# Reciprocal square roots, mask additions and the decay rows' transfers move from GpSimd to VectorE and to the weights' loading queue, in a hybrid decoder block

## The chip, the cores and the metric

The kernel runs on one core of a Trainium2 chip. A core has a matrix engine (TensorE, PE in the profile, with its weight loads as PEld), a vector engine (VectorE, DVE), a scalar engine (ScalarE, ACT), GpSimd (POOL) and SyncE (SP), which issues transfers. Each works off its own instructions in a fixed order and waits for the others by semaphores. The metric is the time of one execution on the device in microseconds (us); less is better.

## The reference

One decoder block over 256 tokens of 2048 channels, in float32: a half-weighted SwiGLU feed-forward, a token mixer, a second feed-forward, a gated per-layer embedding and a last norm.

```python
h = h + 0.5 * swiglu(rmsnorm(h, ffn1_norm), ffn1_w_gate, ffn1_w_up, ffn1_w_down)
proj = rmsnorm(h, mix_norm) @ w_in
o_gdn = gdn_mixer(...)          # 8 heads of 128: convolution, silu, l2norm, gated delta rule, rmsnorm, gate
o_ssm = ssd_mixer(...)          # 16 heads of 64: convolution, silu, chunked state space, gate, rmsnorm
h = h + concat([o_gdn, o_ssm]) @ w_out
h = h + 0.5 * swiglu(rmsnorm(h, ffn2_norm), ffn2_w_gate, ffn2_w_up, ffn2_w_down)
h = h + sigmoid(rmsnorm(h, ple_norm) @ ple_w_gate) * rmsnorm(p @ ple_w_proj, ple_post_norm)
return rmsnorm(h, final_norm)
```

Both mixers need `decay = exp(where(j <= i, gc_i - gc_j, -inf))`, with `gc` the cumulated logs of one head, and the delta rule needs the inverse of a lower triangular matrix `I + lower` per chunk and head. All norms need `x * rsqrt(mean(x * x) + EPS)`.

## The kernel before

**Products.** Weights are stationary. `load` (line 107) brings one column tile of 1 MB through SyncE's queue into one of three buffers `raw`; `split` (line 113) makes a rounded part `hi` on ScalarE (line 118) and the rest `lo` on VectorE (line 119), in pieces of 1024 columns, four buffers each; `chain` (line 122) multiplies both (lines 128, 130, 132), and `total_of` adds the two sums up. This goes on from the first stage to the last. A transfer for `raw` can be issued only when VectorE has made `lo` of the tile that lay there.

**Work beside the products.** The recurrent parts are generators in the list `side`; `tick` (line 174) advances each of them by one step after each piece of a product. The framework then settles the order of each engine's instructions ahead of the run with a simulated timeline; on the chip each engine keeps to that order.

**Per-token scalars** (`scalars`, line 408): at their end the cumulated logs are written as rows to DRAM (`rows<-gct`, line 447, on GpSimd's queue).

**Decay.** `spread` (line 483) loads rows of `gc_i` onto all partitions into one of two buffers `dec` (line 486, GpSimd's queue, 256 KB); `decay` (line 490) adds the causal mask on GpSimd (line 492, 128x512) and exponentiates on ScalarE (line 494). There are 12 of each: one for each of the four pairs of delta-rule heads, two for each of the four quads of state-space heads. A quad also loads `er` twice (line 727, GpSimd's queue, 8 in all).

**Delta rule** (`gdn_pair`, line 500), four pairs in turn. VectorE makes `LA` from `k k^T` and the decay (line 533). The diagonal blocks go through DRAM, on SyncE's queue (`blkl<-LA`, line 554, then `Lb<-blkl`, line 556). GpSimd solves them by substitution in 31 steps of two instructions (`tb`, line 582, and `Z`, line 584); Lb, Z and tb have one buffer. The result goes back through DRAM (`blky<-Z`, line 585, `Y<-blky`, line 592), and VectorE transposes it (`oT<-Y`, line 595). Products on TensorE follow (lines 606 and 635).

**Reciprocal square roots.** `rsq` (line 207) takes the power -0.5 on GpSimd (line 210) and refines it by one Newton step on VectorE (lines 212 to 214). It is called 16 times: six times for the norms over tokens (`stats`, line 220, of `ffn` twice, `mix`, `ple`, `post` and `final`), twice for the state-space groups (`sn`), and twice per pair of delta-rule heads (`rs`, line 543, and `ro`, line 671).

Of the kernel before, what the change touches and what calls it, by code (L numbers as in the profile page):

```python
# [10 lines left out]
F32R = mybir.dt.float32r  # L11
AF = mybir.ActivationFunctionType
# [17 lines left out]
# columns of the parameter pack  # L30
# [12 lines left out]
# the inverse: diagonal blocks of BS, CG columns of one per partition, then doubled  # L43
# [4 lines left out]
# columns of the constant pack: identity, upper triangle, additive causal mask, level masks, unit columns  # L48
# [7 lines left out]
def constant_pack():  # L56
# [5 lines left out]
    # the columns of the identity that the partition holds, partition = (block, group of columns)  # L62
# [6 lines left out]
def tile_hybrid_block(ctx, tc, xT, pT, con, par, wgu1, wd1, wnar, win, wout, wgu2, wd2, wproj, wple, outT):  # L69
# [30 lines left out]
    # ---------------------------------------------------------------- helpers  # L100
# [6 lines left out]
    def load(src):  # L107
        """One transfer of the stationary tiles [P, n * 128] of one column tile."""
        raw = rawp.tile([P, 2048], F32, tag="raw", name="raw")
        nc.sync.dma_start(raw[:, :src.shape[-1]], src)  # L110
        return raw

    def split(src):
        """hi + lo = src exactly, each of them wide enough for one pass."""
# [7 lines left out]
    def chain(ps, hi, lo, act_in, ks, first=True, last=True):  # L122
        """ps[:, 0] (+)= (hi + lo) @ high part, ps[:, 1] (+)= hi @ low part of act_in, for the tiles w of
        hi + lo and the tiles k of act_in."""
# [10 lines left out]
    def single(src, act_in, ks):  # L135
        """The product as a whole in ps[:, 0]."""
# [14 lines left out]
    def product(srcs, act_in, ks, out):  # L151
        """out = the product of the column tile that lies in the transfers srcs, rows ks, with act_in."""
# [18 lines left out]
    # work that runs beside the products: each generator is advanced by one step after each piece  # L171
# [14 lines left out]
    def split_x(k, wname):  # L186
        """The parts of xs are those of h * w, for one k tile."""
# [5 lines left out]
    def split_into(dst, src):  # L193
        """dst[:, :, 0] + dst[:, :, 1] = src exactly."""
        act.copy(dst[:, :, 0, :], src)
        dve.tensor_tensor(out=dst[:, :, 1, :], in0=src, in1=dst[:, :, 0, :].bitcast(F32), op=ALU.subtract)

    def sumsq(acc, src, first):
        """acc[P, 2, T] += src^2, src a pair of tiles."""
# [7 lines left out]
    def rsq(m, n, name):  # L207
        """1/sqrt(m) for a [P, n] tile."""
        y = small.tile([P, n], F32, tag=f"rsq{n}", name=name)
        pool.tensor_tensor(out=y, in0=m, in1=mhalf[:, :n], op=ALU.pow)  # L210
        t = small.tile([P, n], F32, tag=f"rsqt{n}", name=name + "t")
        dve.tensor_tensor(out=t, in0=y, in1=y, op=ALU.mult)
        dve.scalar_tensor_tensor(out=t, in0=t, scalar=-0.5, in1=m, op0=ALU.mult, op1=ALU.mult)
        dve.scalar_tensor_tensor(out=y, in0=t, scalar=1.5, in1=y, op0=ALU.add, op1=ALU.mult)
        return y

    mhalf = cp.tile([P, 16], F32, name="mhalf")
    pool.memset(mhalf, -0.5)

    def stats(squares, width, name, use, wait=2):  # L220
        """use(row): 1/sqrt(mean over width channels + eps) per token, as a row on every partition (in PSUM).
        squares: [P, T] tiles whose sum over partitions and tiles is the sum of squares."""
# [29 lines left out]
    # ---------------------------------------------------------------- loads  # L252
    warm = small.tile([P, 1], F32, tag="warm", name="warm", bufs=1)
    act.activation(warm, ones[:, 0:1], AF.Silu)
    # the array's clock rises with use: multiply while the first transfers are on their way
# [5 lines left out]
    # the first transfers alternate between the tokens and the first three column tiles  # L261
# [28 lines left out]
    # ---------------------------------------------------------------- feed-forward  # L290
    def ffn(wgu, wd, squares, next_name, start=None):
        """h += 0.5 * swiglu(rmsnorm(h)); squares: gives those of h; returns those of the new h."""
# [50 lines left out]
    # ---------------------------------------------------------------- token mixer  # L343
    with ExitStack() as mix:
# [5 lines left out]
        # halved conv weights and bias: silu(2u) = u * (1 + tanh(u))  # L350
# [13 lines left out]
        # a pair of projected tiles, behind three columns of zeros  # L364
# [8 lines left out]
        # ---- per-token scalars: a (8), dt (16), b (8) -> decay logs, dt, beta  # L373
        raw = load(wnar)
        ps = mm_bank("nar")
        for k in range(0, KD, 8):
            # both parts as columns of one stationary tile: rows 0-31 and 32-63 of the product
# [30 lines left out]
        def scalars():  # L408
# [9 lines left out]
            # log(1 + e) = 2 atanh(e / (2 + e))  # L418
# [24 lines left out]
            # the cumulated logs as rows, in DRAM to be spread over the partitions from there  # L443
# [3 lines left out]
            nc.gpsimd.dma_start(rows.rearrange("c n i -> (c n) i"), gct)  # L447
# [6 lines left out]
        # ---- projection of a pair of column tiles, causal conv, silu  # L454
# [18 lines left out]
        def silu_gate(w0):  # L473
            """Twice the silu."""
# [8 lines left out]
        def spread(src):  # L483
            """Rows of gc_i on every partition."""
            d = m2.tile([P, 4, P], F32, tag="dec", name="dec")
            nc.gpsimd.dma_start(d.rearrange("p (c n) i -> p c n i", c=src.shape[0]),  # L486
# [3 lines left out]
        def decay(d, c):  # L490
            """exp(gc_i - gc_j) for j <= i, else 0, as [j, n, i]; d: rows of gc_i, c: columns of -gc_j."""
            pool.tensor_tensor(out=d, in0=d, in1=over(cmask, 4), op=ALU.add)  # L492
# [3 lines left out]
        # scratch for the diagonal blocks and their inverses  # L496
        blocks = [[tc.dram_tile([4 * (P // BS), BS, BS], F32, name=f"blk{n}{i}") for n in "ly"] for i in range(2)]

        # ---- gated delta rule, two heads at a time; matrices in the order (chunk, head)
        def gdn_pair(i, KQ, V):  # L500
# [12 lines left out]
            # squares of k (the diagonal of k k^T) and of q by token  # L513
# [424 lines left out]
def _rows(v):  # L938
    """[n * 128] -> [128, n]."""
    return v.reshape(-1, P).T  # L940
# [61 lines left out]
```

## Time and profile before

| | us |
|---|---|
| median of 3 runs | 2117.88 (2116.24 to 2119.15) |
| span of the profiled execution | 2115.8 |
| TensorE busy | 2064.8 |
| VectorE busy | 1351.4 |
| ScalarE busy | 1047.7 |
| GpSimd busy | 256.7 |

The span runs from the first to the last instruction of one profiled execution. The median is 2.1 us above it. A busy time is the time in which the engine had at least one instruction under way. The mixer lies between about 760 and 1165 us of the span; the feed-forwards lie before and behind it.

### The profile page before, as it was taken

Reading aid. Unit: us, or ns where it says so; the run is one execution under the profiler, and the core shown is the slowest. Engines: PE = TensorE matmul, PEld = TensorE weight load, DVE = VectorE, ACT = ScalarE, POOL = GpSimd, SP = SyncE. Lnnn points to the kernel's source line nnn. Section 1 sums busy time; section 2 is a strip of 40 time slices with the busy share of each in tenths; the row PEclk is TensorE's granted clock in tenths of the full one; section 3 lists DMA queues with packets and bytes.
Section 4 is the critical chain, followed back from the end, with each engine's and each line's share of the span. In section 5 each row is a group of like instructions: output and inputs, shape, how many; then the busy total and the mean of one; then the engine's idle time right before and its main releaser. Section 6 shows DMA issues by size and latency. Waiting matters only on the chain.

```text
span 2115.8 us, 29521 instructions
## 1 busy us (share of the span) xinstructions
PE 2064.8 (98%) x11824; PEld 1795.9 (85%) x11824; DVE 1351.4 (64%) x1908; ACT 1047.7 (50%) x1591; POOL 256.7 (12%) x368
## 2 busy tenths in 40 slices
PE   9999999999999999888989999999999999999997
PEld 7888888888888888777878888888888888888886
DVE  7655555656556677767777666665555556556685
ACT  6444444444445555444455556544444444445554
POOL 2000000000000011667540011000000000000011
PEclk9999999999999999998999999999999999999998
DMA  7555455555545555434544555555456555545652
GB/s 261 187 182 195 158 190 184 207 191 188 182 172 179 190 198 164 163 123 148 168 137 151 194 179 187 191 189 190 163 183 211 185 193 180 190 160 190 201 194 101
DMA packets 67129, 380.77 MB, mean 180 GB/s; under 512 B 11744, under 2 KB 13024, under 8 KB 33840
## 3 DMA queue, kind: packets, MB, share of 16 engines
q1 hardware_dynamic: 65664, 374.93, 52.3%
q0 software_dynamic: 1328, 3.97, 1.0%
q8 instruction: 92, 1.51, 0.3%
q14 instruction: 45, 0.37, 0.1%
HBM read 376.21 MB, written 2.65 MB: 179 GB/s over the span
## 4 chain that ended last, share of the span: by engine, by line
PE 85%; POOL 7%; DMA 3%; issue 2%; DVE 2%; SPq 0%; ACT 0%; POOLq 0%; DVEq 0%; ACTq 0%
PE mm L130 55%; PE mm L128 26%; POOL Z L584 3%; POOL tb L582 3%; PE mm L132 2%; DMA Lb<-blkl 1%; DMA blkl<-LA 1%; DMA er<-rows 1%; DVE lo L119 1%; DMA Y<-blky 0%; PE pj L130 0%; DMA hT<-in_xT 0%; DVE LA L533 0%; POOL dec L486 0%; POOL dec L492 0%
## 5 line engine op out<-in xcount | busy, mean ns | idle before, releaser
L130 PE MATMUL mm<-xs,hi 128*128 128x512 f32 x3888 | 1367.0, 399 | 1.8 <-ACT hi L118 1.8
L119 DVE TENSOR_TENSOR lo<-raw,hi 128x1024 fp32r<-128x1024 f32 (+1 forms) x774 | 864.2, 1124 | 489.8 <-ACT hi L118 489.4
L128 PE MATMUL mm<-xs,lo 128*128 128x256 f32 x3645 | 1028.8, 282 | 6.4 <-DVE lo L119 6.4
L118 ACT CAST hi<-raw 128x1024 fp32r<-128x1024 f32 (+1 forms) x774 | 745.7, 964 | 517.7 <-PE mm L130 403.5
L130 PEld LDWEIGHTS mm<-xs,hi 128*128 128x128 f32 x3888 | 718.5, 189 | 155.9 <-ACT hi L118 2.3
L128 PEld LDWEIGHTS mm<-xs,lo 128*128 128x128 f32 x3645 | 687.5, 189 | 20.8 <-DVE lo L119 8.4
L130 PE MATMUL mm<-hid,hi 128*128 128x512 f32 x1408 | 492.5, 397 | 0.0
L128 PE MATMUL mm<-hid,lo 128*128 128x256 f32 x1344 | 377.8, 281 | 0.0
L130 PEld LDWEIGHTS mm<-hid,hi 128*128 128x128 f32 x1408 | 260.2, 188 | 59.0
L205 POOL TENSOR_TENSOR acc<-acc,sq 128x512 f32<-128x512 f32 x43 | 65.6, 1525 | 1602.3 <-ACT sq L204 1578.0
L128 PEld LDWEIGHTS mm<-hid,lo 128*128 128x128 f32 x1344 | 253.3, 188 | 3.0
L168 ACT COPY t<-mm 128x256 f32<-128x256 f32 x167 | 62.4, 374 | 158.5 <-PE mm L130 157.6
L169 DVE TENSOR_TENSOR t<-t,mm 128x256 f32<-128x256 f32 x167 | 69.9, 419 | 85.7 <-ACT t L168 85.4
L168 ACT COPY s<-mm 128x256 f32<-128x256 f32 x88 | 32.8, 373 | 148.2 <-PE mm L130 148.1
L130 PE MATMUL mm<-osp,hi 128*128 128x512 f32 x256 | 88.9, 396 | 0.0
L169 DVE TENSOR_TENSOR s<-s,mm 128x256 f32<-128x256 f32 x88 | 37.1, 421 | 73.7 <-ACT s L168 73.6
L132 PE MATMUL mm<-xs,lo 128*128 128x256 f32 x243 | 69.6, 286 | 11.7 <-DVE lo L119 11.7
L584 POOL TENSOR_TENSOR Z<-Z,tb 128x124 f32<-128x124 f32 (+30 forms) x124 | 67.8, 547 | 9.4
L128 PE MATMUL mm<-osp,lo 128*128 128x256 f32 x240 | 67.1, 281 | 0.0
L132 PEld LDWEIGHTS mm<-xs,lo 128*128 128x128 f32 x243 | 45.9, 189 | 24.5 <-DVE lo L119 14.1
L582 POOL TENSOR_TENSOR tb<-Lb,Z 128x124 f32<-128x124 f32 (+30 forms) x124 | 61.7, 498 | 27.0 <-DMA Lb<-blkl 17.9
L130 PEld LDWEIGHTS mm<-osp,hi 128*128 128x128 f32 x256 | 46.9, 188 | 10.1
(296 smaller groups left out, 1091.4 us busy)
## 6 DMA issues: line engine op xcount, KB each, us to landing
raw<-in_wgu SPq DMA_DIRECT2D x173, 1024.0 KB, 4.8
raw<-in_wd SPq DMA_DIRECT2D x128, 704.0 KB, 4.1
raw<-in_win SPq DMA_DIRECT2D x52, 1024.0 KB, 5.0
raw<-in_wout SPq DMA_DIRECT2D x16, 1024.0 KB, 4.9
raw<-in_wple SPq DMA_DIRECT2D x16, 1024.0 KB, 4.8
first<-in_wgu SPq DMA_DIRECT2D x12, 256.0 KB, 7.2
dec<-rows POOLq DMA_DIRECT2D x12, 256.0 KB, 4.7
Lb<-blkl SPq DMA_DIRECT2D x4, 512.0 KB, 5.2
```

The source lines that it names most:

```text
L118: act.copy(hi, src)
L119: dve.tensor_tensor(out=lo, in0=src, in1=hi.bitcast(F32), op=ALU.subtract)
L128: pe.matmul(ps[:, 0, :], lo[:, w, :], act_in[:, k, 0, :], start=False, stop=False, skip_group_check=True)
L130: pe.matmul(ps, hi[:, w, :], act_in[:, k], start=start, stop=stop, skip_group_check=True)
L132: pe.matmul(ps[:, 0, :], lo[:, w, :], act_in[:, k, 0, :], start=False, stop=False, skip_group_check=True)
L168: act.copy(out, ps[:, 0, :])
L169: dve.tensor_tensor(out=out, in0=out, in1=ps[:, 1, :], op=ALU.add)
L205: pool.tensor_tensor(out=acc, in0=acc, in1=sq, op=ALU.add)
L582: pool.tensor_tensor(out=t, in0=over(Lb[:, j, j + 1:], CG), in1=Z[:, :, j:j + 1].to_broadcast([P, CG, n]), op=ALU.mult)
L584: pool.tensor_tensor(out=Z[:, :, j + 1:], in0=Z[:, :, j + 1:], in1=t, op=ALU.subtract)
```

## The change

- `rsq` no longer uses GpSimd. A first guess is made on the bits of the number with two VectorE instructions (shift, then subtract from a constant), and three Newton steps of three VectorE instructions follow, in place of one power and one step. The tile `mhalf` and its memset go.
- `decay` adds the mask on VectorE.
- The write of the rows (line 447) and the loads of `dec` (line 486) and `er` (line 727) are issued by SyncE.

The rest of the difference is comments that were taken out.

```diff
 def rsq(m, n, name):
     y = small.tile([P, n], F32, tag=f"rsq{n}", name=name)
-    pool.tensor_tensor(out=y, in0=m, in1=mhalf[:, :n], op=ALU.pow)
     t = small.tile([P, n], F32, tag=f"rsqt{n}", name=name + "t")
-    dve.tensor_tensor(out=t, in0=y, in1=y, op=ALU.mult)
-    dve.scalar_tensor_tensor(out=t, in0=t, scalar=-0.5, in1=m, op0=ALU.mult, op1=ALU.mult)
-    dve.scalar_tensor_tensor(out=y, in0=t, scalar=1.5, in1=y, op0=ALU.add, op1=ALU.mult)
+    dve.tensor_scalar(t.bitcast(I32), m.bitcast(I32), 1, None, op0=ALU.logical_shift_right)
+    dve.tensor_scalar(y.bitcast(I32), t.bitcast(I32), -1.0, float(0x5F3759DF), op0=ALU.mult, op1=ALU.add)
+    for _ in range(3):
+        dve.tensor_tensor(out=t, in0=y, in1=y, op=ALU.mult)
+        dve.scalar_tensor_tensor(out=t, in0=t, scalar=-0.5, in1=m, op0=ALU.mult, op1=ALU.mult)
+        dve.scalar_tensor_tensor(out=y, in0=t, scalar=1.5, in1=y, op0=ALU.add, op1=ALU.mult)
     return y
-mhalf = cp.tile([P, 16], F32, name="mhalf")
-pool.memset(mhalf, -0.5)
...
-    nc.gpsimd.dma_start(rows.rearrange("c n i -> (c n) i"), gct)
+    nc.sync.dma_start(rows.rearrange("c n i -> (c n) i"), gct)
...
 def spread(src):
     d = m2.tile([P, 4, P], F32, tag="dec", name="dec")
-    nc.gpsimd.dma_start(d.rearrange("p (c n) i -> p c n i", c=src.shape[0]),
+    nc.sync.dma_start(d.rearrange("p (c n) i -> p c n i", c=src.shape[0]),
                         src.unsqueeze(0).to_broadcast([P, *src.shape]))
...
 def decay(d, c):
-    pool.tensor_tensor(out=d, in0=d, in1=over(cmask, 4), op=ALU.add)
+    dve.tensor_tensor(out=d, in0=d, in1=over(cmask, 4), op=ALU.add)
...
     for hh in range(2):
-        nc.gpsimd.dma_start(er[64 * hh:64 * hh + 64],
+        nc.sync.dma_start(er[64 * hh:64 * hh + 64],
                             rows[1, 8 + h0:12 + h0, :].rearrange("(j h) l -> h j l", h=2)[hh:hh + 1]
                             .to_broadcast([64, 2, P]))
```

## Rows read from the trace of the kernel before

**Rows 1.** The page, part 1: busy time, share of the span, instructions.
```profile
PE 2064.8 (98%) x11824; PEld 1795.9 (85%) x11824; DVE 1351.4 (64%) x1908; ACT 1047.7 (50%) x1591; POOL 256.7 (12%) x368
```
**Rows 2.** Stretches of the mixer: length, busy per engine, granted clock, DMA share, GB/s.
```profile
800.00:1100.00 300.00, 265.42 (x1587) 230.76 (x1586) 219.67 (x439) 146.23 (x294) 174.47 (x296) 0.94 0.47 148
...
950.00:1000.00 50.00, 39.63 (x236) 34.55 (x237) 34.36 (x66) 23.60 (x51) 34.44 (x61) 0.86 0.48 142
...
996.00:998.00 2.00, 2.00 (x8) 1.64 (x7) 2.00 (x3) 1.38 (x3) 1.83 (x3) 0.50 0.00 0
```
**Rows 3.** Timeline of TensorE: start, length, instruction, idle before it and releaser.
```profile
883.88 0.58 PE L132 MATMUL mm<-xs,lo 128*128 128x256 f32 x1 [9.33 <-DVE lo L119]
...
993.77 1.22 PE L635 MATMUL st<-xv,kd 128*128 128x128 f32 x4 [8.51 <-DVE xv L642]
...
1063.91 1.22 PE L635 MATMUL st<-xv,kd 128*128 128x128 f32 x4 [7.69 <-DVE xv L642]
```
**Rows 4.** Timeline of GpSimd and VectorE at 879 us.
```profile
879.11 1.66 POOL L210 TENSOR_TENSOR rs<-ss,mhalf 128x8 f32<-128x8 f32 x1
...
880.81 0.17 DVE L212 TENSOR_TENSOR rst<-rs 128x8 f32<-128x8 f32 x1 [10.68 <-POOL rs L210]
```
**Rows 5.** Timeline of GpSimd, ScalarE and VectorE at 983 to 992 us.
```profile
983.03 1.33 POOL L486 DMA_DIRECT2D dec<-rows  x2 [0.18 <-issue]
...
988.30 1.26 POOL L492 TENSOR_TENSOR dec<-dec,cont 128x512 f32<-128x512 f32 x1 [2.87 <-DMA dec<-rows]
...
989.60 1.29 ACT L494 ACTIVATE dec<-dec,ngc 128x128 f32<-128x128 f32 x4 [11.74 <-POOL dec L492]
...
991.85 1.53 DVE L119 TENSOR_TENSOR lo<-raw,hi 128x1024 fp32r<-128x1024 f32 x1 [13.18 <-ACT hi L118]
```
**Rows 6.** The chain that ended last: start us, length us, what.
```profile
819.88 9.79 DMA er<-rows
...
894.00 1.22 POOL tb L582
...
934.01 1.53 DMA blky<-Z
...
961.26 0.75 POOL tb L582
...
1006.31 1.53 DMA blky<-Z
```
**Rows 7.** Timeline of VectorE: the transposition behind two of the substitutions.
```profile
943.28 0.71 DVE L595 STREAM_TRANSPOSE oT<-Y 128x512 f32<-128x512 f32 x1 [10.50 <-DMA Y<-blky]
...
1013.99 0.71 DVE L595 STREAM_TRANSPOSE oT<-Y 128x512 f32<-128x512 f32 x1 [3.27 <-DMA Y<-blky]
```
**Rows 8.** Timeline of GpSimd: one substitution instruction, VectorE busy and VectorE idle.
```profile
865.63 1.24 POOL L582 TENSOR_TENSOR tb<-Lb,Z 128x72 f32<-128x72 f32 x1
...
980.58 0.33 POOL L584 TENSOR_TENSOR Z<-Z,tb 128x72 f32<-128x72 f32 x1
```
**Rows 9.** Groups of GpSimd: line, operation, count, busy, mean ns, idle before.
```profile
L492 POOL TENSOR_TENSOR dec<-dec,cont 128x512 f32<-128x512 f32 x12 | 16.2, 1352 | 24.2 <-DMA dec<-rows 24.2
```
**Rows 10.** Timeline of VectorE and GpSimd in the last 30 us.
```profile
2090.93 0.69 DVE L893 TENSOR_TENSOR t<-t,rh 128x512 f32<-128x512 f32 x1
...
2104.55 0.71 POOL L210 TENSOR_TENSOR final<-finalm,mhalf 128x2 f32<-128x2 f32 x1 [7.54 <-DVE finalm L232]
...
2105.29 0.16 DVE L212 TENSOR_TENSOR finalt<-final 128x2 f32<-128x2 f32 x1 [0.82 <-POOL final L210]
...
2105.68 0.16 DVE L214 SCALAR_TENSOR_TENSOR final<-finalt,final 128x2 f32<-128x2 f32 x1
```
**Rows 11.** Who waited for whom: us in total, times, longest us.
```profile
SPq L585 <- POOL Z L584: 52.1, 4, 22.2
...
ACT er L734 <- DMA er<-rows: 11.1, 4, 4.7
```

**Rows 12.** The page, part 6: transfer, queue, count, KB each, median us to landing.
```profile
dec<-rows POOLq DMA_DIRECT2D x12, 256.0 KB, 4.7
```

More of the change, by code (lines that the diff above doesn't have):

```diff
@@ L11 @@
 F32R = mybir.dt.float32r
+I32 = mybir.dt.int32
 AF = mybir.ActivationFunctionType
```

## The prediction

> **What bounds the kernel now.** First the page's busy times: TensorE works 98% of the span, VectorE 64%, GpSimd 12% [rows 1]. By these shares nothing that GpSimd does can matter, so the next view is the table of stretches, to see where the missing 2% lies. TensorE is idle almost only in the mixer: of 300 us it works 265 in 800 to 1100, of 50 us 39.6 in 950 to 1000 [rows 2]. TensorE's timeline then gives each idle time and who ended it. Three are large, 9.33, 8.51 and 7.69 us, all ended by VectorE, 25.5 us together [rows 3]. Behind each the granted clock is low: 0.50 at 996 to 998, the level of 1.2 GHz in place of 2.4 GHz, while TensorE has work [rows 2]. In windows of 2 us such a stretch holds 4 to 6 us of busy TensorE, of which half is lost: 2 to 3 us behind each, some 8 us in all.
>
> Why VectorE was late is read from the other engines at these times. At 880.81 it had waited 10.68 us for the power of line 210 on GpSimd, which had itself waited behind the 62 substitution instructions of the pair before [rows 4]. At 991.85 it had waited 13.18 us for ScalarE, ScalarE 11.74 us for the mask addition on GpSimd, and that one had waited for the load which GpSimd issued only at 983.03, in the middle of a substitution [rows 5]. The idle time at 1063.91 has the same rows behind it, 70 us later. So GpSimd is nowhere busy enough to be a bound, yet its queue is: short steps that others need stand in it behind long ones.
>
> The chain that ended last says what else is in line. From 819 to 1084 us it hardly touches TensorE. It goes from the rows' loads over `LA`, the blocks through DRAM, the substitution (894.0 to 934.0 in the second pair, 961.3 to 1006.3 in the third), back through DRAM and to the transposition [rows 6], behind which VectorE makes the next pair's `LA`. At that transposition VectorE waits 10.50 and 3.27 us already now [rows 7]. This loop is the reason not to book the 25.5 us as gain: when VectorE is no longer held by the power or by the mask, it comes to the transposition earlier and waits there.
>
> **The change part by part.** The sum is made in the profiled execution, 2115.8 us of span, and carried over to the median, 2.1 us above it.
>
> *Power and Newton steps on VectorE.* Each of 16 roots loses one GpSimd instruction and gains eight small ones on VectorE. A small dependent one takes 0.20 us from start to start [rows 10]; where the order interleaves others, less. At the very end of the kernel nothing hides it: from 2104.46, where the mean is ready, to 2105.84 the old root took 1.4 us; the new one takes 11 x 0.195 = 2.15. Cost 0.75 us. (The two instructions on integers aren't in the trace; I give them the 0.16 us of the other small ones, and between 0.1 and 0.5 each the tail moves by under 0.7 us.) The norms of the feed-forward and of the embedding lie beside full TensorE work and cost nothing as long as VectorE has idle time there. In the mixer the root `rs` no longer stands behind a substitution: the wait of 10.68 us goes. What is late next is the transposition of the first pair. In the second pair it starts 9.3 us after the substitution's end (934.0 to 943.28) [rows 6, 7]; in the first the substitution ends at 879.1, where the power starts [rows 4], so `Y` is there at about 886 to 888 whatever VectorE does, and VectorE, freed at 870, waits there instead of at the power. So of 9.33 us much stays. On the loop itself only the power's 1.66 us goes [rows 4]. I take 1.6; the end on the other side is 8, if SyncE's order lets the next pair's blocks out ahead of the write-back.
>
> *The mask on VectorE.* Twelve additions of 1.35 us leave GpSimd [rows 9], twelve of about 0.69 us come to VectorE [rows 10], 8.3 us. Together with about 11 roots in the mixer, at 0.8 to 1.6 us, VectorE gets 17 to 26 us more in a stretch (800 to 1100) where it works 220 us and TensorE 265 [rows 2], some 257 of it without the low clock. It fits, but at over 90% it is no longer a cover for everything, and its order is fixed: a mask addition that waits for its load holds the `lo` pieces behind it, on which TensorE lives. GpSimd waited for these loads 24.2 us in 10 times [rows 9], at no cost; on VectorE such a wait is hidden only by the pieces made ahead, which lasted 4.4 us (from 870.13, where VectorE stopped, to 874.55, where TensorE did) and 6.6 us (978.67 to 985.26) [rows 3 to 5].
>
> *Loads on SyncE.* 21 issues move. None stands behind a substitution instruction any more; they stand in line with weights and with the write-back `blky<-Z`, at which SyncE waited 52.1 us in four times, up to 22.2 [rows 11]. Behind a waiting load stand the weights; three buffers and four pieces ahead have covered gaps of that size: none of the three large idle times stands behind the 22.2 us one [rows 3, 11]. The first loads: `er` took 9.79 us to land [rows 6], and ScalarE waited for `er` in all four quads, 11.1 us [rows 11], the first time ahead of the first `LA`. On SyncE's queue `blky<-Z`, 64 KB like `er`, took 1.53 us [rows 6], so between 0 and 8.3 us of the loop's start go; I take 3, since the transfers also get weights as neighbours in their queue.
>
> *The substitution without interruptions.* In the third pair loads and masks stand between its steps: 1.33 + 2.87 + 1.26 and the second mask and `er`, 7.9 us in all [rows 5]. The second pair's, without interruptions and with a busy VectorE, took 40.0 us, the third 45.0 [rows 6]. So 5 us go, with ends of 0 and 7.9; the fourth pair is like the third.
>
> A rule speaks against part of this, and the rows bear it out. A substitution instruction of 72 columns took 1.24 us with VectorE busy and 0.33 with VectorE idle [rows 8]. The Trainium skill, page SBUF — State Buffer, section Who interferes with whom, says that a VectorE instruction with two inputs in SBUF and a GpSimd instruction that reads SBUF exclude each other for the whole instruction. By that rule each added VectorE instruction with two inputs slows the substitutions, and by a plain count of the interruptions the sum would be 2 x 2.9 us better.
>
> *Sum.* To the third pair's transposition (1014 us) the loop sets the time: -3 -1.6 -5, and +2 for the roots and masks that VectorE now does between transposition and `LA` (two turns, about 1 us each): -7.6. From there to 1084 the loads set it: 7.69 us, about 1 us of smaller waits and 3 us of low clock would go, 11.7; I book half, 6, because the mask additions now wait on VectorE itself. End of the kernel: +0.75. Together -12.85: 2117.88 - 12.85 = 2105.0.
>
> **The rivals.** *All of it goes.* If the new order brings the next pair's `LA` ahead of the transposition, the loop no longer binds, and the 25.5 us and the 8 us of clock go: 2117.9 - 33.5 + 0.75 = 2085. For it: the two stand close in the program. Against: VectorE at over 90%.
>
> *Given back.* VectorE waits at transposition and masks as long as it did for GpSimd: the loop's -1.6 and half of one substitution remain, 2117.9 - 1.6 - 2.5 + 0.75 = 2114.6, to 2120 with 5 us of longer substitutions by the contention above. For it: [rows 7] and [rows 8].
>
> *Slower: loads behind the write-back.* The loads of the third and fourth pair's stretch were issued in the middle of a substitution [rows 5]. If SyncE's order puts them behind that pair's `blky<-Z`, they go out at its end, at about 1002 instead of 983, and land 4.7 us later [rows 12]; the mask comes at 1007 instead of 992. VectorE then reaches the transposition about 12 us later than now, twice: 2117.9 + 24 - 4.6 + 0.75 = 2138. It decides from the point where the buffer of `dec` comes free, in the simulated order, after the substitution's end. Against it: GpSimd's order had the issues at half of the substitution.
>
> **How the numbers follow.** The forecast 0.46 (2097 to 2113), all of it 0.22 (2085), given back 0.19 (2114 to 2121), slower 0.13 (2138). Predicted is the forecast, 2105. The range reaches to the first rival and over the second: 2085 to 2122. A measurement of this kernel can tell 0.2%, 4.2 us, from no change: faster 0.68, same 0.18, slower 0.14.
>
> **What would show it.** After the change no row may have VectorE wait for GpSimd at line 212, and no load of `dec` may start between substitution steps on GpSimd. The idle time at 883 should shrink and be ended by the transposition's wait; the waits of [rows 7] should be longer; the third and fourth substitutions should last about 40 us. Wrong would be: a substitution as long as before, VectorE waiting for `dec` loads by 10 us, or weights late behind SyncE's waits.

## The result, and the profile after

| | before | after |
|---|---|---|
| median, us | 2118.5 (2116.2 to 2120.9) | 2137.0 (2135.4 to 2138.5) |
| span of the profiled execution, us | 2115.8 | 2133.3 |
| TensorE idle in the span (span less busy time), us | 51.0 | 65.4 |

The ratio after to before is 1.0084 (1.0070 to 1.0099): slower by 18.5 us, where 13 us less was forecast. First the page's busy times after, which answer [rows 1], and two stretches (length; busy times of PE, PEld, DVE, ACT and POOL with their instructions; granted clock; DMA share; GB/s), which answer [rows 2].

```profile
PE 2067.9 (97%) x11824; PEld 1796.4 (84%) x11824; DVE 1369.3 (64%) x2048; ACT 1044.6 (49%) x1591; POOL 204.8 (10%) x318
...
800.00:1100.00 300.00, 259.78 (x1529) 224.98 (x1528) 221.90 (x489) 143.33 (x282) 129.44 (x256) 0.93 0.46 146
1100.00:1200.00 100.00, 92.53 (x561) 81.08 (x561) 75.59 (x155) 51.05 (x92) 3.46 (x4) 0.97 0.45 151
```

GpSimd lost 52 us of work and VectorE gained 18, as the change says. TensorE works 5.6 us less in 800 to 1100, at nearly the same granted clock (0.93 for 0.94), and it is idle for 7.5 us in 1100 to 1200, where it was not idle at all before:

```profile
1100.00:1200.00 100.00, 100.00 (x599) 87.93 (x598) 75.11 (x119) 56.30 (x92) 8.15 (x8) 1.00 0.51 175
```

TensorE's timeline names the large ones (start, length, instruction, idle before it and its releaser); the first three answer [rows 3]:

```profile
887.98 0.66 PE L606 MATMUL ip<-oT,LA 128*128 128x64 f32 x2 [13.31 <-DVE rst L216]
...
1004.19 1.22 PE L635 MATMUL y<-xv,Y 128*128 128x128 f32 x4 [7.92 <-DVE Y L611]
...
1086.07 0.66 PE L759 MATMUL py<-dec,xd 128*64 128x128 f32 x2 [8.07 <-issue]
...
1173.76 1.35 PE L679 MATMUL ot<-cont,o 128*128 128x128 f32 x4 [5.41 <-ACT o L674]
1177.18 0.80 PE L131 MATMUL mm<-osp,hi 128*128 128x512 f32 x1 [2.06 <-DVE osp L197]
```

The three large idle times of before are still there, at other instructions, and two at the end of the mixer are new. The last row is the first product of the output projection. Before, it began at 1162.27, and nothing waited:

```profile
1162.27 0.40 PE L130 MATMUL mm<-osp,hi 128*128 128x512 f32 x1
```

So 14.9 of the span's 17.5 us have come together by the end of the mixer. The four transpositions in VectorE's timeline, which answer [rows 7], show from which turn on:

```profile
887.12 0.71 DVE L595 STREAM_TRANSPOSE oT<-Y 128x512 f32<-128x512 f32 x1 [13.74 <-DMA Y<-blky]
...
943.76 0.71 DVE L595 STREAM_TRANSPOSE oT<-Y 128x512 f32<-128x512 f32 x1 [2.20 <-DMA Y<-blky]
...
1026.58 0.70 DVE L595 STREAM_TRANSPOSE oT<-Y 128x512 f32<-128x512 f32 x1
...
1104.27 0.70 DVE L595 STREAM_TRANSPOSE oT<-Y 128x512 f32<-128x512 f32 x1
```

The second is where it was (943.28 before [rows 7]). The third is 12.6 us late (1013.99 before [rows 7]) and waits for nothing on VectorE. What lies between is the second pair's chain of products, and in it one root. The root `ro` of the first pair has twelve instructions now, with the product behind it (line 672). These are seven of them in VectorE's timeline, the first five and the last two:

```profile
950.53 0.16 DVE L212 TENSOR_SCALAR rot<-rq 128x4 int32<-128x4 int32 x1
951.88 0.16 DVE L213 TENSOR_SCALAR ro<-rot 128x4 int32<-128x4 int32 x1
954.26 0.15 DVE L215 TENSOR_TENSOR rot<-ro 128x4 f32<-128x4 f32 x1
955.88 0.15 DVE L216 SCALAR_TENSOR_TENSOR rot<-rot,rq 128x4 f32<-128x4 f32 x1
957.17 0.15 DVE L217 SCALAR_TENSOR_TENSOR ro<-rot,ro 128x4 f32<-128x4 f32 x1
...
964.63 0.38 DVE L217 SCALAR_TENSOR_TENSOR ro<-rot,ro 128x4 f32<-128x4 f32 x1
967.30 0.34 DVE L672 TENSOR_TENSOR ro<-ro,rq 128x4 f32<-128x4 f32 x1
```

And before:

```profile
951.43 0.16 DVE L212 TENSOR_TENSOR rot<-ro 128x4 f32<-128x4 f32 x1
952.71 0.16 DVE L213 SCALAR_TENSOR_TENSOR rot<-rot,rq 128x4 f32<-128x4 f32 x1
952.92 0.15 DVE L214 SCALAR_TENSOR_TENSOR ro<-rot,ro 128x4 f32<-128x4 f32 x1
953.39 0.16 DVE L672 TENSOR_TENSOR ro<-ro,rq 128x4 f32<-128x4 f32 x1
```

Each small instruction takes 0.16 us, but from one to the next of the same root it is 0.5 to 2.7 us, since VectorE's settled order has other work between them. The root lasts 17 us and is ready 13.9 us later than before. TensorE shows who stands behind it. Its order has the first pair's output transpositions (`ot`, line 679), which need the root, ahead of the second pair's first product of the doubling (`ip`, line 606). That product, before and then after:

```profile
956.26 0.33 PE L606 MATMUL ip<-oT,LA 128*128 128x64 f32 x2
```

```profile
969.65 0.33 PE L606 MATMUL ip<-oT,LA 128*128 128x64 f32 x2
```

It is 13.4 us later. The first of these `ot` says what TensorE did in the meantime:

```profile
968.39 0.33 PE L679 MATMUL ot<-cont,o 128*128 128x128 f32 x1 [0.91 <-ACT o L674]
```

It waited only 0.91 us there; products that the order puts ahead of `ot` fill the time. So at this place the length of the root acts through the order that was settled ahead of the run, and hardly as a wait of TensorE. What the delay costs shows later, in the third transposition and at the mixer's end.

The third rival's mechanism is there as well. In SyncE's timeline after the change, a load of `dec` goes out right behind the write-back for which SyncE had waited, and VectorE waits for it at the mask:

```profile
997.27 0.33 SPq L585 DMA_DIRECT2D blky<-Z  x1
997.64 0.43 SPq L486 DMA_DIRECT2D dec<-rows  x1
```

```profile
1002.73 0.69 DVE L492 TENSOR_TENSOR dec<-dec,cont 128x512 f32<-128x512 f32 x1 [9.12 <-DMA dec<-rows]
```

At 1080.28 the same happens with `er`, behind the write-back of 1079.86: ScalarE waits 14.03 us for it, the decay behind it on ScalarE is late, and TensorE is idle for 8.07 us. So there were two candidates for the loss: the roots' chain, and transfers held in SyncE's queue.

### The profile page after: what moved, and what is told of

The parts are those of the page before. It is cut to its first block, busy times and chain, and to the rows that moved or that the text cites. A ratio compares the mean times of both kernels' runs of the same rounds, so it can differ in the third digit from the quotient of the medians.

```text
span 2133.3 us, 29603 instructions
## 1 busy us (share of the span) xinstructions
PE 2067.9 (97%) x11824; PEld 1796.4 (84%) x11824; DVE 1369.3 (64%) x2048; ACT 1044.6 (49%) x1591; POOL 204.8 (10%) x318
## 4 chain that ended last, share of the span: by engine, by line
PE 87%; POOL 6%; DMA 4%; DVE 2%; issue 1%; SPq 1%; ACT 0%; DVEq 0%; POOLq 0%; ACTq 0%
PE mm L131 56%; PE mm L129 27%; POOL Z L584 3%; POOL tb L582 3%; PE mm L133 2%; DMA Lb<-blkl 1%; DMA blkl<-LA 0%; DMA dec<-rows 0%; DMA first<-in_wgu 0%; PE pj L131 0%; DMA raw<-in_wgu 0%; DMA Y<-blky 0%; DMA raw<-in_win 0%; DVE lo L120 0%; DVE LA L533 0%
## 5 line engine op out<-in xcount | busy, mean ns | idle before, releaser
L129 PEld LDWEIGHTS mm<-xs,lo 128*128 128x128 f32 x3645 | 692.1, 190 | 20.5 <-DVE lo L120 9.2
L584 POOL TENSOR_TENSOR Z<-Z,tb 128x124 f32<-128x124 f32 (+30 forms) x124 | 63.3, 511 | 9.7
```

Of the source, the lines that this page charges most:

```text
L129: pe.matmul(ps[:, 0, :], lo[:, w, :], act_in[:, k, 0, :], start=False, stop=False, skip_group_check=True)
L584: pool.tensor_tensor(out=Z[:, :, j + 1:], in0=Z[:, :, j + 1:], in1=t, op=ALU.subtract)
```

## Experiments: one part at a time

The theory at this point was the third rival, transfers held behind the write-back (held transfers for short), against two others. Each kernel is the one before with one part of the change, or two. The diffs are the parts of the diff above.

> From the kernel before, only the reciprocal square roots move to VectorE; masks and transfers stay on GpSimd. Held-transfer theory (the loss of the whole change comes from transfers that stand behind the write-back of the substitution on SyncE): no harm here, the 10.7 us wait for the power goes and 1.6 to 9 us of it come out at the end less 0.75 us in the tail: 2110 to 2118 us. VectorE theory (added small instructions on VectorE delay the pieces): eight instructions more per root, about eleven roots in the mixer, 1 to 1.6 us each: 2125 to 2135 us. Single-buffer theory (an earlier transposition changes the settled order, and the buffer of Y, which GpSimd clears only after the pair before has used it, then holds the next pair): slower than before although no transfer moved, and GpSimd waits over 10 us at the clearing of Y in the third pair.

> From the kernel before, only the mask additions move to VectorE; roots and transfers stay on GpSimd. Held-transfer theory: the loads start as before, in the middle of a substitution, and the mask no longer waits for GpSimd, so no harm: 2112 to 2119 us. VectorE theory: twelve additions of about 0.7 us and their waits for loads now hold the pieces on VectorE: 2125 to 2132 us, with waits of VectorE for the transfers of dec of 5 us or more ahead of idle times of TensorE. Single-buffer theory: the order of the third pair stays, so nothing, 2116 to 2120 us.

> From the kernel before, only the transfers of the decay rows move to SyncE; roots and masks stay on GpSimd. In this kernel's settled order the transfers of the first quad beside the third substitution stand ahead of that pair's write-back, not behind it as in the whole change. Held-transfer theory as first stated (any move to SyncE costs because transfers stand behind write-backs): 2130 to 2140 us. If instead only a transfer that really stands behind a write-back costs, and here none of the third pair does: 2110 to 2120 us, the third substitution about 40 us long. VectorE theory: VectorE has no instruction more, so 2112 to 2119 us.

> Roots and mask additions on VectorE, transfers left on GpSimd, that is the whole change with the transfers put back. Held-transfer theory: the loss is gone, the time is 2105 to 2118 us. VectorE theory: the loss stays, 2130 to 2140 us. Single-buffer theory: the clearing of Y for the third pair waits over 10 us again, and the time lies between, 2120 to 2132 us.

| | us | ratio to before, interval |
|---|---|---|
| roots alone | 2133.1 | 1.0077 (1.0062 to 1.0092) |
| masks alone | 2117.5 | 0.9998 (0.9989 to 1.0008) |
| transfers alone | 2122.1 | 1.0021 (1.0011 to 1.0030) |
| roots and masks | 2131.8 | 1.0072 (1.0057 to 1.0087) |

The roots alone make 15.6 us of loss, with every transfer where it was. So held transfers can't be the cause of the whole loss. Both kernels with the roots lie in the range of the theory that the added instructions load VectorE (2125 to 2135 and 2130 to 2140 us). But the 2117.5 of the masks alone speak against a load in general: twelve additions and their waits for `dec` cost nothing. The single buffer of Y is seen (GpSimd waits 14.2 us to clear it with the roots alone, 23.0 in the whole change), but it waits for the products of the pair before, which are late themselves; it passes the delay on. The transfers alone cost 4.5 us, between the ranges that were expected.

## Experiments: the chain of the root

New theory: a root costs by its length in dependent instructions, since the order puts pieces of the splitting between them, and others stand behind it. The table below gives, beside the times, how many `lo` instructions (line 119) come ahead of the third and fourth transposition on VectorE, counted in the traces. The expectations count otherwise (304 and 320 for the kernel before, where its trace has 378 and 394; what they start from isn't known), and the shifts differ too: all roots on VectorE come out 4 and 5 pieces later and not 7, the two short chains (e8 and e5) one piece earlier and not 3 to 5. The edits, each made in the kernel before unless it says otherwise:

```diff
 # e5: guess only (in the kernel with the roots alone)
-    for _ in range(3):
+    for _ in range(0):
 # e6: power on GpSimd, then three Newton steps on VectorE
+    for _ in range(3):
         dve.tensor_tensor(out=t, in0=y, in1=y, op=ALU.mult)
...
 # e7: in the kernel with the roots alone
-WAIT = 9
+WAIT = 10
 # e8: power on GpSimd, the Newton step taken out
-    dve.tensor_tensor(out=t, in0=y, in1=y, op=ALU.mult)
-    dve.scalar_tensor_tensor(out=t, in0=t, scalar=-0.5, in1=m, op0=ALU.mult, op1=ALU.mult)
-    dve.scalar_tensor_tensor(out=y, in0=t, scalar=1.5, in1=y, op0=ALU.add, op1=ALU.mult)
 # e11: the new root where name is "rs" or "ro", the old one elsewhere
+    if name in ('rs', 'ro'):
```

> Roots on VectorE as in the run with roots alone, but the guess stands without any Newton step: 2 dependent instructions in place of 11 (so the norms are off by some per cent; this part of the computation is left out). Masks and transfers are as before. Chain theory: the root costs because its 11 dependent instructions are settled one behind each piece of VectorE's splitting, which takes them 3 to 6 pieces of some 3.3 us. With two instructions the third and fourth transposition stand 301 and 316 pieces into VectorE's order (311 and 327 with the full root, 304 and 320 before): the loss is gone, 2104 to 2118 us. Rival, leaving GpSimd is what costs (VectorE then comes too early to the first transposition and waits there for the substitution): that wait stays, 13 us or more, and the time is 2128 to 2135 us.

> The kernel before with the power left on GpSimd, but three Newton steps behind it in place of one: nine dependent instructions on VectorE, six more than before. Masks and transfers are as before. Chain theory: the third and fourth transposition move from 304 and 320 pieces into VectorE's order to 308 and 325, and the time rises by about 4 to 5 pieces of 3.3 us: 2129 to 2135 us, nearly that of the full root on VectorE. Rival, leaving GpSimd is what costs: power and its place behind the substitution are as before, so only the small instructions' own time is added, 2117 to 2121 us.

> The run with roots alone on VectorE, and one constant changed: the transposition stands ten steps of the side work behind the write-back in place of nine. The instructions are the same, only their settled order differs: the third and fourth transposition come at 307 and 324 pieces into VectorE's order in place of 311 and 327. Chain and order theory: about 3 pieces of 3.3 us come back, 2121 to 2128 us. Rival, VectorE's added instructions cost by the time they take: nothing comes back, 2130 to 2136 us.

> The kernel before with the power on GpSimd and no Newton step behind it. Masks and transfers are as before. Chain theory: the chain is shorter by three dependent instructions than before, and the third and fourth transposition move from 304 and 320 pieces to 300 and 315: the time falls by up to 4 pieces of 3.3 us, 2104 to 2114 us, unless the substitution sets the turn (then 2114 to 2118 us). Rival, the chain on VectorE plays no part: 2117 to 2118 us.

> The kernel before, with only the two roots of each pair of delta-rule heads (rs and ro, 8 of 16 calls) on VectorE; the norms keep the power on GpSimd, masks and transfers are as before. Chain theory: these are the roots that the turns wait for, the third and fourth transposition stand at 308 and 324 pieces (304 and 320 before, 311 and 327 with all roots): most of the loss, 2124 to 2132 us. Rival, the norms' roots (mix above all, at the start of the turns) are what is late: 2116 to 2121 us.

| | dependent VectorE instructions per root | `lo` ahead of third, fourth transposition | us | ratio, interval |
|---|---|---|---|---|
| before | 3 | 378, 394 | 2118 | |
| no step, power on GpSimd (e8) | 0 | 377, 393 | 2113.4 | 0.9979 (0.9970 to 0.9989) |
| guess only (e5) | 2 | 377, 393 | 2118.9 | 1.0005 (0.9996 to 1.0015) |
| three steps, power on GpSimd (e6) | 9 | 381, 398 | 2129.7 | 1.0054 (1.0036 to 1.0072) |
| only `rs` and `ro` (e11) | 11 | 382, 399 | 2129.1 | 1.0052 (1.0035 to 1.0069) |
| all roots, WAIT = 10 (e7) | 11 | 379, 397 | 2128.8 | 1.0050 (1.0034 to 1.0066) |
| all roots (e1) | 11 | 382, 399 | 2133.1 | 1.0077 (1.0062 to 1.0092) |

The pair e5 and e6 decides. With the roots off GpSimd and a short chain the loss is gone (2118.9, 0.9 us above the range of the chain theory and 9 below that of its rival). With the power left on GpSimd and a long chain, 12.0 us of the 15.6 are there. So it is not leaving GpSimd that costs, nor the place of the root, but for the most part the length of the chain. The rival's wait at the first transposition is in e5 as well (14.12 us), and costs nothing there. The two roots of the pairs alone make 11.1 us. WAIT = 10 gives 4.4 us back, with the same instructions, 0.8 us short of the expected range; the two intervals overlap a little, so this one is weak. A chain that is shorter still gives 4.3 us (e8), but e5, with the same count, gives nothing, and e1 and e11 have one count and 4.0 us between them: the count shows the direction and not the microseconds.

Then the link itself. In TensorE's order `ip` stands behind `ot`, and `ot` behind the root. Two steps more ahead of `ot` take the link away, in the whole change and, as the control, in the kernel before:

```diff
-            for _ in range(4):
+            for _ in range(6):
                 yield
             ps = mx_bank("ot")
```

> The whole change, and one constant: the transposition of a pair's outputs (the one that waits for the root ro) stands six steps of the side work behind the root in place of four. All instructions are the same. Chain theory with its link: the loss comes since, in TensorE's fixed order, the next pair's first product of the doubling stands behind this transposition, and so behind the root. With two steps more the third and fourth transposition of Y stand at 307 and 322 pieces into VectorE's order (311 and 326 in the whole change): 8 to 14 us come back, 2122 to 2129 us. Rival, transfers held behind the write-back on SyncE: they stay where they are, 2133 to 2139 us.

> The kernel before with the same constant changed, six steps in place of four between the root ro and the output's transposition; nothing of the change is in it. Chain theory: the root behind the transposition is short here, so little stands to be gained by the link, yet the order moves a little forward (302 and 318 pieces in place of 304 and 320): 2108 to 2118 us. Rival, the two steps help any kernel alike by moving work elsewhere, and say nothing about the root: the gain is as large as in the whole change, 8 us or more, below 2110 us.

The whole change falls from 2137.0 to 2122.7 us (ratio to before 1.0022, 1.0012 to 1.0032). The kernel before stays: 2119.1 (1.0007, 0.9997 to 1.0017), 1.1 us above the range expected of the chain theory, so the edit is no gain for every kernel. All instructions of the whole change are still there, and 14.3 us of its time are gone: so much of the loss is not the time that the added instructions take on VectorE. Three rows of the whole change with it, the first and third of TensorE, the second of VectorE:

```profile
949.83 1.00 PE L606 MATMUL ip<-oT,LA 128*128 128x64 f32 x8
```

```profile
964.07 0.15 DVE L672 TENSOR_TENSOR ro<-ro,rq 128x4 f32<-128x4 f32 x1
```

```profile
965.36 0.27 PE L679 MATMUL ot<-cont,o 128*128 128x128 f32 x1
```

The root is still long (13.6 us, ready at 964.07), but the second pair's `ip` no longer stands behind it: 949.83 in place of 969.65. The third transposition comes at 1015.83 in place of 1026.58, with 378 `lo` ahead of it, as many as before the change.

## Experiments: the write-back in SyncE's queue

What the transfers cost beside this is tested from the other side: leave them on SyncE, and take away what they stand behind.

```diff
-            nc.sync.dma_start(by.rearrange("q c i -> (q c i)").rearrange("(p f) -> p f", p=P),
+            nc.gpsimd.dma_start(by.rearrange("q c i -> (q c i)").rearrange("(p f) -> p f", p=P),
                               Z.rearrange("p c i -> p (c i)"))
...
-                nc.sync.dma_start(Y[p, :, p], by.rearrange("(m b) c i -> b c m i", m=4)[q])
+                nc.gpsimd.dma_start(Y[p, :, p], by.rearrange("(m b) c i -> b c m i", m=4)[q])
```

> The whole change, and the write-back of the substitution and the loads of Y behind it are issued by GpSimd, so that no transfer of the decay rows and no weight stands behind a wait for a substitution on SyncE. The settled order of the third and fourth transposition is 312 and 327 pieces, one more than in the whole change. Held-transfer theory as the cause of the whole loss: 2112 to 2122 us. As the cause of the small rest that the chain theory leaves (the whole change against roots and masks without the transfers, some 5 us): 2129 to 2134 us. Neither: 2135 to 2142 us.

This was a surprise: 2108.0 us (0.9951, 0.9936 to 0.9966), 29 us under the whole change, though the roots' chain is still in it and the third and fourth transposition have 383 and 399 `lo` ahead of them, no fewer than in any kernel above. It is below even the range for held transfers as the cause of everything, which the first four runs had excluded. So the same edit went into the kernel before, and into the change without its roots; and both remedies were put together.

> The kernel before, and only the write-back of the substitution and the loads of Y behind it are issued by GpSimd in place of SyncE. Held-queue theory in the form that belongs to this change (the moved transfers of the decay rows are what is held on SyncE): here they are still on GpSimd, in the middle of the substitutions, so little changes: 2113 to 2120 us. Rival, the weights held behind the write-back are what costs in every kernel: 8 us or more are gained here too, 2090 to 2110 us.

> Mask additions on VectorE and transfers on SyncE, roots left on GpSimd: the whole change without the roots. Chain theory: the loss is gone but for what the transfers alone cost, 2115 to 2124 us. If transfers held behind the write-back cost by themselves as much as the roots: 2128 to 2136 us. Third possibility, the gain that was forecast for the whole change appears once the roots' chain is away: 2100 to 2112 us.

> Masks on VectorE, transfers on SyncE, roots left on GpSimd, and the write-back and the loads of Y issued by GpSimd. If the two causes are separate, the stalls of TensorE that the transfers ended (7 to 8 us twice, and the low clock behind them) and the roots' chain are both gone: 2090 to 2106 us, less than the whole change with the write-back moved (2108). If the root on GpSimd then stands behind the substitution and is waited for again, as before: 2106 to 2116 us.

> The whole change with both remedies: write-back and loads of Y issued by GpSimd, and the output's transposition six steps behind the root in place of four. If the causes add up (14 us for the second remedy alone, 29 us for the first alone), 2094 to 2104 us; if the second remedy only helped by moving work away from the held transfers, nothing more is gained: 2105 to 2111 us.

| | write-back on SyncE | write-back on GpSimd | difference |
|---|---|---|---|
| the kernel before | 2118.0 | 2109.0 (e13) | -9 |
| masks and transfers | 2118.3 (e14) | 2092.4 (e15) | -26 |
| the whole change | 2137.0 | 2108.0 (e12) | -29 |
| the whole change, `ot` two steps later | 2122.7 (e9) | 2098.7 (e16) | -24 |

Read downwards, the roots (third row less second) cost 18.7 and 15.6 us, nearly the same in both columns. Masks and transfers (second less first) bring nothing in the left column and 16.6 us in the right one. So the two causes are separate. The roots' chain is a loss in both columns; held transfers are no loss against before, but they take a gain away: loads that GpSimd held in the middle of a substitution are now held by SyncE at the end of one. VectorE's waits for `dec` (us in total, times, longest), first with masks and transfers, then with the write-back moved too:

```profile
DVE dec L492 <- DMA dec<-rows: 24.0, 8, 12.0
```

```profile
DVE dec L492 <- DMA dec<-rows: 12.8, 8, 2.9
```

And TensorE's idle times of over 5 us in the two, in the same order:

```profile
882.80 1.94 PE L606 MATMUL ip<-oT,LA 128*128 128x64 f32 x8 [12.12 <-DVE oT L595]
...
1009.88 1.23 PE L635 MATMUL o<-xv,LA 128*128 128x128 f32 x4 [5.32 <-DVE xv L658]
...
1081.08 0.80 PE L635 MATMUL o<-xv,LA 128*128 128x128 f32 x2 [8.64 <-DVE xv L658]
```

```profile
889.70 0.66 PE L606 MATMUL ip<-oT,LA 128*128 128x64 f32 x2 [13.74 <-DVE oT L595]
```

The second and third idle time are gone; the first pair's wait for its substitution stays. The traces of masks and transfers show what was held in each of the two. Ahead of the third, SyncE's and VectorE's timelines have decay rows, issued behind the write-back of 1069.80:

```profile
1070.71 0.84 SPq L486 DMA_DIRECT2D dec<-rows  x2
```

```profile
1076.00 0.69 DVE L492 TENSOR_TENSOR dec<-dec,cont 128x512 f32<-128x512 f32 x1 [11.99 <-DMA dec<-rows]
```

Ahead of the second, they have weights: three transfers go out at once behind the write-back of 1000.27, ScalarE waits 10.89 us for one of them, and VectorE for ScalarE.

```profile
1000.70 1.33 SPq L110 DMA_DIRECT2D raw<-in_win  x3
```

```profile
1007.93 1.23 DVE L119 TENSOR_TENSOR lo<-raw,hi 128x1024 fp32r<-128x1024 f32 x1 [10.70 <-ACT hi L118]
```

With the write-back moved, ScalarE waits for no weight in the mixer. In 800 to 1100 TensorE is idle for 33.3 us with masks and transfers and for 16.1 with the write-back moved too, 17.3 less, and the granted clock there is 0.93 and 0.97; on 284 us of work these 0.04 are some 11 us, an estimate. Together that is about the difference of the two spans, 27.6 us.

So not only the decay rows are held. The kernel before has them on GpSimd and gains 9 us as well (2109.0), in the range of the rival in its expectation, weights held in every kernel. Its trace shows them: two weights go out at 934.43, right behind the write-back of 934.01, and ScalarE waits 8.49 us for one; with the write-back moved this wait is gone. That it makes all of the 9 us is not shown. Two last runs asked what the 26 us are, and whether more is left.

```diff
 # e17: masks on VectorE, roots on GpSimd, write-back on SyncE; rows<-gct, dec and er:
-    nc.sync.dma_start(...)
+    nc.scalar.dma_start(...)
 # e18: e15, without the Newton step behind the power, and range(6) ahead of ot
```

> Masks on VectorE, roots left on GpSimd, and the transfers of the decay rows issued by ScalarE: neither behind a substitution nor behind the write-back, which stays on SyncE with weights and blocks behind it. If the rows held behind the write-back are what takes the gain of masks and transfers away: 2098 to 2108 us. If the weights and the next pair's blocks held there are: 2115 to 2121 us, as with the transfers on SyncE.

> Masks on VectorE, rows on SyncE, write-back and loads of Y issued by GpSimd, the power on GpSimd with no Newton step behind it, and the output's transposition six steps behind the root. If the length of the chain behind the root still sets part of the turns: 2080 to 2090 us, below the 2092 us of the same with one Newton step and four steps. If the first pair's wait for its substitution (13.7 us of idle TensorE) is all that is left, 2090 to 2096 us.

With the rows on ScalarE's queue it is 2112.9 us (0.9973, 0.9963 to 0.9982), between the two ranges: 5 of the 26 us. In its trace the rows are no longer held, VectorE waits for `dec` 11.3 us in eight times, up to 3.6; in place of it VectorE waits 43.6 us at the four transpositions for the loads of Y, which are still issued behind the write-back (25.7 us with the transfers on SyncE, 19.5 with the write-back moved). The rest of the 26 us is then held with other things behind the write-back, that is weights, the next pair's blocks and the loads of Y, or it is paid in ScalarE's queue. The traces name single waits, as above, but no run divides the microseconds among them. e18 is 2094.6 (0.9886, 0.9868 to 0.9904), no better than e15 (0.9894, 0.9866 to 0.9923): with the other two causes away a shorter chain with `ot` two steps later brings nothing, and of the idle times the first pair's wait (10.26 us there) is the large one left. e15, masks on VectorE, rows on SyncE, roots as before and the write-back on GpSimd, is the fastest of all: 25.7 us under before, 44.6 under the change.

## Why the prediction was wrong, step by step

*The step that failed: the root in the mixer.* The prediction priced eight more small instructions as busy time, 0.8 to 1.6 us per root, and took the 0.20 us from start to start of the kernel's last root, where nothing else was left to do. The end of the kernel came out as it said: from the mean to the first product of the row 1.82 us before (2104.08 to 2105.90) and 2.60 after (2120.59 to 2123.19), 0.78 for 0.75. In the mixer the root `ro` of the first pair takes 17 us for 12 instructions. In the sum this is the term "+2 for the roots and masks", about 1 us in each of two turns: one such root was 13.9 us later and the third transposition 12.6, and in the kernel's time the roots cost 15.6 us by themselves (e1) and 18.7 in the whole change (against e14). So the term is mis-sized by a factor of about ten, and behind it stands a missed dependency: no sentence asked who stands behind `ro`. The trace of before had the hint, in the root whose start stands in [rows 4]: its second and third instruction come 1.7 and 1.8 us behind the one ahead.

```profile
880.81 0.17 DVE L212 TENSOR_TENSOR rst<-rs 128x8 f32<-128x8 f32 x1 [10.68 <-POOL rs L210]
...
882.53 0.16 DVE L213 SCALAR_TENSOR_TENSOR rst<-rst,ss 128x8 f32<-128x8 f32 x1
...
884.34 0.16 DVE L214 SCALAR_TENSOR_TENSOR rs<-rst,rs 128x8 f32<-128x8 f32 x1
```

Eight links more at some 1.5 us make 12 us, an estimate from the distances above, which is about the 13.9 measured.

*The power.* Right: the wait for GpSimd at the root is gone, and what is late next is the transposition of the first pair, at 887.12 (13.74 us of waiting) where the prediction put its `Y` at 886 to 888. The warning that much of the 9.33 us stays was too mild; the idle time is now 13.31 us.

*The masks.* Right in price, 12 x 0.69 us (the median of one is 693 ns), and right that they would wait for loads: 20.5 us in seven times, up to 9.1. By themselves they cost nothing (e2).

*The loads.* Put at 3 us of gain at the start of the loop. The first substitution begins at 844.0 in place of 845.4, and at 840.0 with the transfers alone. Behind that, what was named as the third rival's condition came true at 997.64 and 1080.28, and the 6 us booked for the later idle times did not come: they are 7.92 and 8.07 us, before 8.51 and 7.69. The prediction also read from [rows 3, 11] that three buffers and four pieces ahead cover the weights behind a waiting write-back. No large idle time stood there, but behind the 22.2 us wait of [rows 11] ScalarE had waited 8.49 us for a weight already before the change, as said above.

*The substitution.* Right in direction, and more than was booked: the third and fourth lasted 33.2 and 33.5 us in place of 45.0 and 46.6. The gain was off the path. The third pair's substitution ended at 997.2, but its Y could be cleared only when the second pair's products were done:

```profile
1022.20 0.53 POOL L590 MEMSET Y<- 128x512 f32 x1 [23.00 <-PE y L635]
```

Part of this shortness is a symptom: VectorE stood idle beside it. The stretches of the fourth substitution in the whole change and in e15:

```profile
1046.30:1079.80 33.50, 29.09 (x198) 25.47 (x197) 20.21 (x40) 11.27 (x21) 28.72 (x62) 1.00 0.39 126
```

```profile
1016.50:1057.00 40.50, 40.50 (x282) 35.78 (x280) 36.40 (x64) 24.07 (x52) 35.72 (x62) 1.00 0.51 169
```

With VectorE busy for 20.21 of 33.50 us the 62 instructions took 33.5 us; with 36.40 of 40.50 they took 40.5, in a kernel 45 us faster. This agrees with the rule of the Trainium skill that the prediction weighed (SBUF — State Buffer, Who interferes with whom), in direction; no run here separates it from other causes.

*The rivals.* The third rival's figure, 2138, is within 1 us of the time, but for the most part by another cause. Its mechanism is in the trace twice, yet putting the transfers back on GpSimd gives only 5 us back (2137.0 against 2131.8), while taking the roots out gives 18.7. What its mechanism did is keep the forecast gain from showing: 16.6 us, against the 14 us that the sum had for transfers, substitutions and the later idle times (3 + 5 + 6). The time of the first rival, all idle time gone at 2085, is nearly reached by e15 (2092.4), but only with the write-back out of the way and the roots back on GpSimd, and with 13.74 us of idle time left at the first pair.

## What to carry to other kernels

Price a step that is made of dependent small instructions by the distance from one to the next in the busiest stretch, not by their length or by their distance where the engine has nothing else to do; then ask which instruction of each other engine stands behind its result. When a transfer moves to another queue, ask what that queue waits for and not how full it is: a wait for a long substitution holds whatever stands behind it, and the gain of a change can hide there. Test a change of several parts by part and also with the suspected holder taken away, since a part that shows nothing by itself (masks and transfers, 0 us) may be worth 17.

## What the runs showed of the hardware

Two things were not expected. Issuing the write-back and the loads of Y from GpSimd is slower for the write-back itself and faster for the kernel. The median to landing of `blky<-Z` is 1.5 us on SyncE and 2.3 on GpSimd (e15), and one issue takes 0.33 and 0.65 us; the kernels are 9 to 29 us faster. The Trainium skill (DMA: Bandwidth & Descriptors, Issuing engines are not separate DMA queues) says that starting transfers from several engines only saves the time that the sequencer takes to start them. The 20 issues in question take SyncE 8 us in the kernel before (4 of 0.33 and 16 of 0.43 us), less than each of the gains; here the measurement decides. What is saved is the wait in front of the issue, 64.7 us in four times in the whole change:

```profile
SPq L585 <- POOL Z L584: 64.7, 4, 22.5
```

The other is how much a few small instructions can cost through an order: 11 to 19 us in each of five comparisons (e1, e6, e11, and the two columns above), although the instructions that were added take 0.16 us each and VectorE's share of busy time stayed at 64%. With `ot` two steps later the same instructions cost 4 to 6 us (e9 against e14, e16 against e15).
